# Down projection as seven half-size products with weight sums made in DRAM, and the out projection as four pairs of products, in a hybrid decoder block

## The chip, the cores and the metric

One core of one Trainium2 chip. The metric is the device time of one execution in microseconds, the median of several runs. TensorE (PE) multiplies, VectorE (DVE), ScalarE (ACT) and GpSimd (POOL) work element by element, SyncE (SP) issues most of the transfers; POOL issues the accumulating ones.

## The reference

A decoder block on 512 tokens with 16 learned meta tokens ahead, D = 1024, feed-forward width 2816. Two token mixers run in parallel (mLSTM and gated linear attention) and are merged by gates; then come an output projection, a second norm and a SwiGLU channel mixer. All products are asked for in float32. What matters here:

```python
xn = rmsnorm(h, norm1_g); proj = xn @ w_in        # mq mk mv mi mf mo gq gk gv ga gr gate_m gate_g
y_m = head_rmsnorm(mlstm_chunkwise(...)) * sigmoid(mo)
y_g = head_rmsnorm(gla_chunked(...)) * silu(gr)
merged = sigmoid(gate_m) * (y_m @ w_branch_m) + sigmoid(gate_g) * (y_g @ w_branch_g)
h = h + merged @ w_out
hn = rmsnorm(h, norm2_g)
ff = silu(hn @ w_ff_gate) * (hn @ w_ff_up)
h = h + ff @ w_ff_down
out = rmsnorm(h, final_g)
```

## The kernel before

Channels lie on the 128 partitions and tokens along the free dimension, so a tile of activations is 128 x 512 (or 528 with the meta tokens). A float32 product is made in three passes: weights and activations are each split into a high part (rounded by a cast on ACT) and a low part (the difference, on DVE), and high x high, high x low and low x high are summed in PSUM (`mm3`, L307 to L312).

Weights come in units of 128 x 1024 (512 KB, eight k-tiles of one output tile of 128 channels), loaded by SP (`load_raw`, L189) some units ahead into four buffers. `whi` (L196, ACT) and `wlo` (L201, DVE) split them. When a unit begins, `begin` (L279) hands out by tables (PLAIN, FIRST, SECOND) which splits of later units are emitted after which k-tile of the present one. Every other piece of work (norms, mixers, evacuations) is a Python generator in a list: `tick()` (L161), called after each k-tile, advances each by one step, and the number that it yields is how many ticks it then skips. So the order of the instructions on each engine is that of the program text, and the yields set it.

There are two kinds of job. A plain unit (`unit`, L316) makes one output tile with 24 matmuls of 512 columns. A pair (`pair`, L361, `seven`, L350) makes two output tiles by a scheme of the kind of Strassen's: with the weights as 2 x 2 blocks and the activations as 2 x 2 blocks, seven products of sums (q1, q5, q6, p2, p3, p4, p7), each half the size in k and in columns, 84 matmuls of 128 x 256 in all. p3 of a pair runs inside the next one. The sums of weights for pairs are made by accumulating DMAs that POOL issues (L191 into `raw`, L220 into `wf`) and by DVE (`s2` L235, `s4` L247); sums of the evacuated products are made by ACT and DVE, through a table of closures that a sink returns.

The stages: gates and mLSTM projections as plain units (0 to about 200 us); gates, GLA and the mLSTM's output as pairs, the branch units bm, and the mixers beside them (to about 480); eight branch units bg, whose result times gate plus the mLSTM's branch is the merged tile (`branch`, L1191 to L1204, to about 522); eight plain units out with the residual, the gain and the sum of squares behind each (L1358 to L1370, to about 568); the second norm (L1383), and, since all of the normed activations and their sums are needed (`operands`, L1416 to L1467), four plain gate and up units and then 18 pairs fg/fu with SwiGLU (L1488 to L1496, to about 792); the down projection, and the tail.

The down projection before takes 22 units of 512 KB, whose eight blocks of 128 x 128 follow a fixed list (output tiles 0 and 1 in turn for each of the 22 k-tiles, then tiles 2 to 7 one after the other). The activations are split once (L1525). Tiles 0 to 6 are 22 x 3 matmuls of 512 columns, tile 7 is done in two halves of 256 columns; after each tile its result is subtracted from the residual (L1570, the up branch carries a minus sign), squared for the last norm, and scaled by the gain. `final` (L1588) sums the squares over partitions by a matmul with ones, takes the root, and scales and stores the half that is done.

## Time and profile before

| | us |
|---|---|
| runs | 928.77 median of 3 (928.13 to 928.81) |
| the profiled execution | 928.98, its span 927.2 |
| PE busy | 912.5 (6145 matmuls in the record) |
| DVE busy | 631.0 |
| ACT busy | 539.0 |
| POOL busy | 90.4 |
| mean granted clock of PE | 0.995 |

A row of the groups gives line, engine, operation, output and inputs by name, shape and count, then busy us, mean ns of one, and the idle time ahead of it with what ended it. The waits list what PE waited for, with the total, the number and the longest in us. A row of a timeline has start, duration, engine, line and operation. The windows give busy us of each engine in a stretch, then the granted clock of PE (1.00 is full), the share of the 16 DMA engines' time that was used, and GB/s.

### The profile page before, as it was taken

How to read it: one execution, taken by the hardware profiler on the slowest of the kernel's cores; microseconds unless marked ns; L12 is line 12 of the kernel's file. 1: busy time of each engine (PE TensorE's matmuls, PEld its weight loads, DVE VectorE, ACT ScalarE, POOL GpSimd, SP SyncE). 2: the span in 40 equal slices, each digit the busy share in tenths (PEclk: the TensorE clock that was granted, in tenths of full speed). 3: DMA queues.
4: the chain of work that ended last, by engine and by line, in shares of the span. 5: the costliest groups of instructions: out<-in, count | busy, mean ns of one | idle time of the engine just before them, and what ended most of it. 6: DMA issues, size and time to landing. Idle time of an engine off the chain costs nothing.

```text
span 927.2 us, 15643 instructions
## 1 busy us (share of the span) xinstructions
PE 912.5 (98%) x6145; PEld 842.9 (91%) x6145; DVE 631.0 (68%) x937; ACT 539.0 (58%) x959; POOL 90.4 (10%) x109
## 2 busy tenths in 40 slices
PE   9999999999999999999999999999999999999995
PEld 9889999899998899999998888889999999888885
DVE  4889676888865487777786554997766767822323
ACT  6667568898774276767683334455555556722222
POOL 0000021111100011011100000141111210000000
PEclk9999999999999999999999999999999999999998
DMA  9255374465643567556543443357676775432302
GB/s 345 97 167 146 126 165 104 104 147 139 162 124 91 129 157 168 147 128 159 137 123 94 130 148 109 80 137 193 172 203 183 174 188 152 136 92 68 114 1 92
DMA packets 50650, 128.21 MB, mean 138 GB/s; under 512 B 5616, under 2 KB 11888, under 8 KB 50576
## 3 DMA queue, kind: packets, MB, share of 16 engines
q1 hardware_dynamic: 36224, 103.96, 35.4%
q0 software_dynamic: 13120, 22.16, 15.4%
q10 hardware_dynamic: 1232, 1.09, 0.4%
q8 instruction: 48, 0.79, 0.3%
q14 instruction: 26, 0.21, 0.1%
HBM read 121.82 MB, written 5.37 MB: 137 GB/s over the span
## 4 chain that ended last, share of the span: by engine, by line
PE 92%; DVE 5%; ACT 2%; issue 1%; DVEq 0%; POOL 0%; POOLq 0%
PE b L310 14%; PE b L312 14%; PE b L311 14%; PE b L356 14%; PE b L358 14%; PE b L357 14%; ACT t L140 1%; PE b L1153 1%; PE b L1152 1%; DVE wlo L201 1%; DVE t L1439 1%; PE b L1132 1%; PE b L824 1%; DVE hx L1446 1%; PE b L1173 1%
## 5 line engine op out<-in xcount | busy, mean ns | idle before, releaser
L311 PE MATMUL b<-t,whi 128*128 128x512 f32 (+2 forms) x790 | 277.4, 351 | 0.2 <-DVE t L925 0.2
L356 PE MATMUL b<-t,whi 128*128 128x256 f32 (+1 forms) x912 | 261.5, 287 | 0.9 <-ACT t L417 0.5
L310 PE MATMUL b<-t,whi 128*128 128x512 f32 (+2 forms) x742 | 261.1, 352 | 0.0
L312 PE MATMUL b<-t,wlo 128*128 128x512 f32 (+2 forms) x742 | 258.4, 348 | 2.2 <-DVE wlo L201 2.2
L358 PE MATMUL b<-t,wlo 128*128 128x256 f32 (+1 forms) x912 | 257.8, 283 | 0.7 <-DVE wlo L201 0.7
L357 PE MATMUL b<-t,whi 128*128 128x256 f32 (+1 forms) x912 | 257.3, 282 | 0.0
L201 DVE TENSOR_TENSOR wlo<-raw,whi 128x1024 fp32r<-128x1024 f32 x153 | 187.7, 1229 | 95.3 <-ACT whi L196 94.9
L196 ACT CAST whi<-raw 128x1024 fp32r<-128x1024 f32 x153 | 160.4, 1052 | 59.7 <-PE b L357 27.4
L356 PEld LDWEIGHTS b<-t,whi 128*128 128x128 f32 x912 | 171.9, 188 | 1.9 <-ACT t L417 0.8
L358 PEld LDWEIGHTS b<-t,wlo 128*128 128x128 f32 x912 | 171.7, 188 | 0.9 <-DVE wlo L201 0.9
L357 PEld LDWEIGHTS b<-t,whi 128*128 128x128 f32 x912 | 172.0, 189 | 0.4
L311 PEld LDWEIGHTS b<-t,whi 128*128 128x128 f32 x790 | 149.6, 189 | 20.8 <-DVE t L925 0.8
L312 PEld LDWEIGHTS b<-t,wlo 128*128 128x128 f32 x742 | 140.6, 189 | 21.0 <-DVE wlo L201 2.6
L310 PEld LDWEIGHTS b<-t,whi 128*128 128x128 f32 x742 | 140.8, 190 | 18.6
L140 ACT ACTIVATE t<-t 128x512 f32<-128x512 f32 (+7 forms) x133 | 76.1, 589 | 44.7 <-DVE t L1195 25.5
L191 POOL DMA_DIRECT2D raw<-wst x38 | 32.9, 866 | 369.8 <-DMA wf<-wst 122.6
L196 ACT CAST whi<-wf 128x1024 fp32r<-128x1024 f32 x38 | 40.0, 1053 | 19.9 <-PE b L357 15.4
L140 ACT ACTIVATE t<-f 128x256 f32<-128x256 f32 (+1 forms) x24 | 11.5, 481 | 62.0 <-DVE f L1570 62.0
L220 POOL DMA_DIRECT2D wf<-wst x38 | 37.4, 993 | 100.4 <-ACT whi L196 41.0
L201 DVE TENSOR_TENSOR wlo<-wf,whi 128x1024 fp32r<-128x1024 f32 x38 | 46.3, 1220 | 0.0
L1492 ACT COPY t<-b 128x256 f32<-128x256 f32 x54 | 18.5, 375 | 43.4 <-PE b L358 43.4
L356 PE MATMUL b<-t,wgh 128*128 128x256 f32 (+1 forms) x152 | 43.2, 284 | 0.0
(248 smaller groups left out, 1194.1 us busy)
## 6 DMA issues: line engine op xcount, KB each, us to landing
raw<-wst SPq DMA_DIRECT2D x153, 512.0 KB, 3.9
wf<-wst SPq DMA_DIRECT2D x38, 256.0 KB, 3.4
wf<-wst POOLq DMA_DIRECT2D x38, 256.0 KB, 6.3
raw<-wst POOLq DMA_DIRECT2D x38, 256.0 KB, 4.2
t<-xT SPq DMA_DIRECT2D x8, 264.0 KB, 5.3
pos<-t SPq DMA_DIRECT2D x8, 264.0 KB, 3.2
xt<-xr SPq DMA_DIRECT2D x4, 512.0 KB, 8.3
t<-xT SPq DMA_DIRECT2D x8, 256.0 KB, 3.9
```

What stands on the lines that cost most here:

```text
L140: S.activation(o, i, func, **kw)
L191: G.dma_start(lr(r, 0), lr(wst[v - 1], 0), accum_op=ALU.add)
L196: S.copy(t, src)
L201: V.tensor_tensor(t, src, hi.bitcast(F32), ALU.subtract)
L220: G.dma_start(lr(st.f, 1), lr(wst[u + 1], 1), accum_op=ALU.add)
L310: T.matmul(o, w_h, ah[:, c0:c1], start=first, stop=False)
L311: T.matmul(o, w_h, al[:, c0:c1], start=False, stop=False)
L312: T.matmul(o, w_l, ah[:, c0:c1], start=False, stop=last)
L356: T.matmul(o, h, xh_[k][:, c0:c1], start=start and k == 0, stop=False, skip_group_check=not start)
L357: T.matmul(o, h, xl_[k][:, c0:c1], start=False, stop=False, skip_group_check=not start)
L358: T.matmul(o, l, xh_[k][:, c0:c1], start=False, stop=k == 3, skip_group_check=not start)
L1492: s7=lambda: S.copy(s[:, lo], bz), s1=lambda: S.copy(s[:, hi], bx), s2=lambda: S.copy(r[:, lo], bx),
```

## The change

Out projection: the eight plain units become four pairs, of output tiles 2i and 2i+1. The merged tiles therefore have to be summed and split into seven operands (`upper_mix`, `lower_mix`, run behind the branch units, which now go 0, 4, 1, 5, 2, 6, 3, 7). The first pair goes over k = 0 to 2 of q1, p7 and p2 first, and then over k = 3. The residual's input is loaded a pair ahead, and sums of squares of four tiles are made by POOL with accumulating DMAs.

Down projection: one such scheme over the whole matrix. With two halves of the 22 k-tiles, of the tokens, and even against odd output tiles, there are seven products, each run for all four pairs of output tiles (4 x 11 x 3 matmuls of 256 columns) before the next. The result of each is added to or subtracted from the residual where it belongs, and three products accumulate into the banks of earlier ones. The activations' sums are made in place on DVE, one product ahead (`make_sum`), and split for each product (`make_op`). The weights come in 44 chunks of two k-tiles for all four pairs, each 512 KB or, at the odd end and for p3, 640 or 768 columns or half. The sums of weights are not made beside the use: `down_sums` makes them in DRAM, in 30 steps, each a copy from DRAM to DRAM (SP) and one job later an accumulating DMA (POOL). A step is advanced at each pair and at each odd bm or bg job, the rest in feed-forward pairs. The last twelve, for p3, pick rows of 512 B.

Many yields elsewhere have other numbers; the arithmetic there is the same.

```diff
@@ gate_rows, conv
         S.copy(gam[:96], gsb[:96])
...
-        yield 1
+        yield 2
...
         while not norm[0]:
-            yield 1
+            yield 6
...
+ORDER = ("q1", "q5", "p2", "p7", "q6", "p4", "p3")
+CHUNKS = [(n, 0, k, min(2, FH - k)) for n in ORDER[:-1] for k in range(0, FH, 2)] + [
+    ("p3", i, k, n) for i in range(4) for k, n in ((0, 6), (6, 5))]
...
+    def down_sums():
+        def plus(dst, a, b):
+            nc.sync.dma_start(dst, a)
+            yield
+            G.dma_start(dst, b, accum_op=ALU.add, max_dma_last_dim=8192)
+
+        for n, a, b in (("q5", wdn[2], wdn[3]), ("p7", wdn[2], wdn[0]), ("q6", dsum["q5"], wdn[0])):
+            for k in range(0, FH, 2):
+                c = slice(k, min(k + 2, FH))
+                yield from plus(dsum[n][c], a[c], b[c])
+        for i in range(4):
+            for k in range(0, FH, 4):
+                c = slice(k, min(k + 4, FH))
+                rows = lambda s: s[c, :, i * P:(i + 1) * P].rearrange("k p n -> p k n")
+                yield from plus(dsum["p3"][i].rearrange("p (k n) -> p k n", k=FH)[:, c], rows(dsum["q6"]), rows(wdn[1]))
...
+        if what in ("bm", "bg") and i % 2 or len(job) == 2:
+            next(sums, None)
...
+    def lower_mix(k):
+        b, b1, c = mo[k + 4].v, mo[k].v, mo[k].c
+        h = tt(F32R, NS)
+        act(h, b, AF.Copy, scale=0.5)
+        t = c[:, R2]
+        V.tensor_tensor(t, b[:, R2], b1[:, R2], ALU.subtract)
+        d = tt(n=NS)
+        V.scalar_tensor_tensor(d[:, L2], c[:, L2], -1.0, b[:, R2], ALU.mult, ALU.subtract)
...
+        lower(l, b, h)
+        put(("p2", "p3"), h, l)
+        V.scalar_tensor_tensor(d[:, R2], d[:, L2], -1.0, b[:, L2], ALU.mult, ALU.subtract)
...
+        lower(p_, t, p)
+        put(("p7",), p, p_)
+        yield 2
+        lower(dl, d, dh)
+        put(("q6", "p4"), dh, dl)
...
+        if last_k:
+            for b, n in ((bx, "q1"), (bz, "p7"), (by, "p2")):
+                seven(b, w, x, n, True, quiet, *cols, range(3))
+            while len(x["p7"][1]) < 4:
+                tick()
+            seven(bx, w, x, "q1", True, quiet, *cols, (3,))
+            e.pop("s1")()
+            mine["p3", 0] = ["s7"]
+            seven(by, w, x, "p2", True, quiet, *cols, (3,))
+            seven(bz, w, x, "p7", True, hook, *cols, (3,))
...
+            return dict(
+                s1=lambda: V.tensor_tensor(s[:, lo], bx, xa[:, lo], ALU.add),
+                s7=lambda: S.copy(s[:, hi], bz),
+                s2=lambda: V.tensor_tensor(r[:, lo], bx, xb[:, lo], ALU.subtract),
+                s5=lambda: V.tensor_tensor(r[:, hi], bx, xb[:, hi], ALU.subtract),
+                c21=lambda: minus(b[:, lo], bz, r[:, lo]),
+                c11=lambda: V.tensor_tensor(a[:, lo], by, s[:, lo], ALU.add),
+                c22=lambda: minus(b[:, hi], s[:, hi], r[:, hi]),
+                c12=lambda: V.tensor_tensor(a[:, hi], bx, xa[:, hi], ALU.add), fin=fin)
...
+    for i in range(4):
+        pair((("out", 2 * i), ("out", 2 * i + 1)), mg, (0, 256), sink_out(2 * i), i == 0)
...
-    for m in range(2, 7):
-        o = bank()
-        down(o, m, 0, NS)
-        run(out_res(m, o, 0, NS))
...
+    def make_op(n, k, part):
...
+        if part == 0:
+            make_sum(n, k)
+        elif part == 1:
+            xd[n][k] = tt(F32R, NS)
+            S.copy(xd[n][k][:, LO], src)
+        else:
+            V.tensor_tensor(xd[n][k][:, HI], src, xd[n][k][:, LO].bitcast(F32), ALU.subtract)
...
+    EVAC = {"q1": [(E, LO, -1, False)], "q5": [(O, HI, 1, False)], "p2": [(E, LO, -1, True)],
+            "p7": [(O, HI, 1, False)], "q6": [(E, HI, -1, False), (O, LO, 1, False), (O, HI, 1, True)],
+            "p4": [(O, LO, 1, True)], "p3": [(E, HI, -1, True)]}
+    INTO = {"q6": "q1", "p4": "p7", "p3": "q5"}
...
+        for step, (ws, xs_) in enumerate(((0, LO), (0, HI), (1, LO))):
+            T.matmul(o, w[ws][:, j * P:(j + 1) * P], xd[n][k][:, xs_], start=fresh and step == 0,
+                     stop=step == 2 and k == FH - 1, skip_group_check=True)
```

How the order moves, at three places. First DVE near the start, in the opening: `wlo` is the low part of the weight that PE uses about 44 us into the span; the narrow operations of 32 partitions belong to the gates' rows, the ones with `pr` and 528 or 512 columns to the convolution. Before:

```order
L678 TENSOR_TENSOR t_83_492<-b_65_410,t_41_183 128x512
L717 TENSOR_TENSOR a2s_343<-pr_69,a2s_343 32x512
L718 SCALAR_TENSOR_TENSOR t_78_462<-t_71_444,pr_69,t_77_461 32x528
L722 COPY t_85_510<-t_77_461 32x4
L723 SCALAR_TENSOR_TENSOR t_76_460<-t_85_510,t_78_462 32x528
L786 SCALAR_TENSOR_TENSOR t_73_454<-t_70_440,pr_69,t_73_454 128x512
L729 TENSOR_TENSOR t_87_524<-t_76_460,t_77_461 32x528
L730 TENSOR_SCALAR t_87_524<-t_87_524 32x528
L786 SCALAR_TENSOR_TENSOR t_79_464<-t_72_447,pr_69,t_79_464 128x528
L201 TENSOR_TENSOR wlo_88_535<-raw_58_232,whi_84_508 128x1024
```

The same place now (L833 is the convolution's L786, L220 is L201, L764 to L777 are L717 to L730):

```order
L833 SCALAR_TENSOR_TENSOR t_82_486<-t_78_467,pr_69,t_82_486 128x528
L220 TENSOR_TENSOR wlo_85_526<-raw_58_236,whi_84_507 128x1024
L833 SCALAR_TENSOR_TENSOR t_72_457<-t_70_444,pr_69,t_72_457 128x512
L764 TENSOR_TENSOR a2s_347<-pr_69,a2s_347 32x512
L765 SCALAR_TENSOR_TENSOR t_77_465<-t_71_448,pr_69,t_76_464 32x528
L769 COPY t_86_537<-t_76_464 32x4
L770 SCALAR_TENSOR_TENSOR t_75_463<-t_86_537,t_77_465 32x528
L776 TENSOR_TENSOR t_88_548<-t_75_463,t_76_464 32x528
L777 TENSOR_SCALAR t_88_548<-t_88_548 32x528
L833 SCALAR_TENSOR_TENSOR t_82_486<-t_78_467,pr_69,t_82_486 128x528
```

The low part has moved ahead of eight rows. Second, DVE where the down projection runs: before, in its first tiles, only low parts of activations of 512 columns and of weights.

```order
L1525 TENSOR_TENSOR t_1577_9160<-t_1248_6940,t_1575_9150 128x512
L1525 TENSOR_TENSOR t_1579_9170<-t_1267_7068,t_1578_9162 128x512
L1525 TENSOR_TENSOR t_1582_9182<-t_1286_7196,t_1580_9172 128x512
L1525 TENSOR_TENSOR t_1585_9194<-t_1305_7324,t_1583_9184 128x512
L201 TENSOR_TENSOR wlo_1587_9201<-raw_1545_8976,whi_1584_9189 128x1024
L1525 TENSOR_TENSOR t_1588_9206<-t_1324_7452,t_1586_9196 128x512
```

Now, in its first product, the sums for the next (L1672), their low parts (L1690), the weights' low parts, and at the end the evacuation into the residual (L1740):

```order
L1690 TENSOR_TENSOR t_1649_9643<-t_1323_7432,t_1649_9643 128x256
L1672 TENSOR_TENSOR t_1361_7688<-t_1361_7688 128x256
L1690 TENSOR_TENSOR t_1651_9661<-t_1342_7560,t_1651_9661 128x256
L1672 TENSOR_TENSOR t_1380_7816<-t_1380_7816 128x256
L220 TENSOR_TENSOR wlo_1655_9693<-raw_1642_9590,whi_1653_9675 128x1024
L1690 TENSOR_TENSOR t_1654_9681<-t_1361_7688,t_1654_9681 128x256
L1672 TENSOR_TENSOR t_1399_7944<-t_1399_7944 128x256
L1690 TENSOR_TENSOR t_1656_9699<-t_1380_7816,t_1656_9699 128x256
L220 TENSOR_TENSOR wlo_1660_9724<-raw_1647_9628,whi_1658_9713 128x1024
L1690 TENSOR_TENSOR t_1659_9719<-t_1399_7944,t_1659_9719 128x256
L1740 TENSOR_TENSOR f_1094_6237<-f_1094_6237,b_1627_9493 128x256
L220 TENSOR_TENSOR wlo_1666_9754<-raw_1652_9666,whi_1664_9737 128x1024
```

Between the weights' low parts, which keep their distance of a few rows, DVE now makes a sum and a low part of 256 columns for each k-tile. Third, POOL's queue at the pairs, before:

```order
L191 DMA raw_403_2271<-wst 128x512
L220 DMA wf_424_2334<-wst 128x512
L191 DMA raw_444_2448<-wst 128x512
L220 DMA wf_453_2477<-wst 128x512
L191 DMA raw_467_2607<-wst 128x512
```

and now, with the accumulating DMAs of the sums (L1222) between the weights':

```order
L198 DMA raw_408_2288<-wst 128x512
L239 DMA wf_424_2339<-wst 128x512
L1222 DMA sum_q5_191<-wdn 64x2048
L198 DMA raw_444_2455<-wst 128x512
L239 DMA wf_453_2484<-wst 128x512
L1222 DMA sum_q5_191<-wdn 64x2048
L198 DMA raw_467_2616<-wst 128x512
```

The copies that these add to (L1220) stand in the same manner between the loads on SP's queue.

More of the change, by code (lines that the diff above doesn't have):

```diff
@@ L108, in hybrid_block @@
 @with_exitstack
-def hybrid_block(ctx: ExitStack, tc: tile.TileContext, xT, xr, wst, par, con, out):
+def hybrid_block(ctx: ExitStack, tc: tile.TileContext, xT, xr, wst, wdn, par, con, out):
     nc = tc.nc
@@ L348, in hybrid_block, with seven @@
     SEVEN = ("q1", "q5", "q6", "p2", "p3", "p4", "p7")
-    def seven(o, w, x, n, start, hook, c0, c1):
+    def seven(o, w, x, n, start, hook, c0, c1, ks=range(4)):
         wh, wl = w[n]
         xh_, xl_ = x[n]
-        for k in range(4):
+        for k in ks:
             h, l = wh[:, k * P:(k + 1) * P], wl[:, k * P:(k + 1) * P]
@@ L754, in gate_rows @@
             yield 2
-        yield 11
+        yield 9
         pst = bank()
@@ L1198, in branch @@
         sg.v = None
-        yield 2
-        if parts is not None:
-            hi, lo = tt(F32R, NS), tt(F32R, NS)
-            act(hi, t, AF.Copy, scale=0.5)
-            yield 4
-            V.scalar_tensor_tensor(lo, t, 0.5, hi.bitcast(F32), ALU.mult, ALU.subtract)
-            parts[0].append(hi)
-            parts[1].append(lo)
-            box.v = None
+        if then is not None:
+            yield from then
+        yield 1
     ym, yg = [None] * 8, [None] * 8
@@ L1212, in hybrid_block @@
     gm, gg = [box() for _ in range(8)], [box() for _ in range(8)]
-    mg = [], []
+    mg = {n: ([], []) for n in SEVEN}
+    mo = [box() for _ in range(8)]
     heads = {}
@@ L1332, in hybrid_block @@
         elif what == "bg":
-            run(branch(box(), branch_unit(job[0], yg), gg[i], merged[i], mg))
-    while side:
-        tick()
+            if i == 3:
+                load_x(0)
+            run(branch(mo[i], branch_unit(job[0], yg), gg[i], merged[i],
+                       upper_mix(i) if i < 4 else lower_mix(i - 4)))
     del ym, yg, xh, xl, gts
@@ L1590, in final, with evac_out @@
+    INTO = {"q6": "q1", "p4": "p7", "p3": "q5"}
+    def evac_out(n, i):
+        for f, c, sign, last in EVAC[n]:
+            update(f(i), c, n, i, sign, last)
+            yield 2
+    def final(a):
+        while hsum[a].n < 8 - a:
+            yield 1
+        yield 1
         ps = bank()[:, :HS]
         for c in (slice(0, P), slice(P, HS)):
-            T.matmul(ps[:, c], ones, hsum[a].v[:, c], start=c.start == 0, stop=False, skip_group_check=True)
-        while o.v is None:
-            yield 1
@@ L1595, in final @@
-        yield from out_res(7, o.v, a * HS, (a + 1) * HS)
-        yield 1
-        for c in (slice(0, P), slice(P, HS)):
-            T.matmul(ps[:, c], ones, hsum[a].w[:, c], start=False, stop=True, skip_group_check=True)
+            T.matmul(ps[:, c], ones, hsum[a].v[:, c], start=c.start == 0, stop=a == 0, skip_group_check=True)
+        if a == 1:
+            while hsum[1].w is None:
+                yield 4
+            yield 9
+            for c in (slice(0, P), slice(P, HS)):
+                T.matmul(ps[:, c], ones, hsum[a].w[:, c], start=False, stop=True, skip_group_check=True)
@@ L1614, in final @@
             yield 1
[L1616 to L1635 removed]
+    flat = [0]
@@ new lines, in down_block @@
+    def down_block(n, i, k, cur):
+        o = out_of(n, i)
+        w = cur.w
+        j = cur.at
+        fresh = n not in INTO and k == 0 and i % 2 == 0
+        for step, (ws, xs_) in enumerate(((0, LO), (0, HI), (1, LO))):
+            T.matmul(o, w[ws][:, j * P:(j + 1) * P], xd[n][k][:, xs_], start=fresh and step == 0,
+                     stop=step == 2 and k == FH - 1, skip_group_check=True)
+        for f in cur.steps.get(j, ()):
+            f()
+        cur.at += 1
+        flat[0] += 1
+        if flat[0] % 2 == 0:
+            tick()
@@ new lines, in hybrid_block, with next_chunk, evac_all_out @@
+    unit_no = [0]
+    def next_chunk():
+        cur = Box()
+        name, _, _, size = CHUNKS[unit_no[0]]
+        u, steps = begin(("down", unit_no[0]))
+        top = (size if name == "p3" else 4 * size) - 1
+        cur.steps = {}
+        for at, fs in steps.items():
+            cur.steps.setdefault(min(at, top), []).extend(fs)
+        unit_no[0] += 1
+        cur.w, cur.at = splits.pop(u), 0
+        return cur
+    def evac_all_out(n):
+        for i in range(4):
+            yield from evac_out(n, i)
@@ new lines, in hybrid_block @@
+    for x, n in enumerate(ORDER):
+        if n in INTO:
+            acc[n] = acc.pop(INTO[n])
+        else:
+            acc[n] = [bank(), bank()]
+        nxt = ORDER[x + 1] if x + 1 < len(ORDER) else None
+        if n != "p3":
+            for k in range(FH):
+                if k % 2 == 0:
+                    cur = next_chunk()
+                for i in range(4):
+                    down_block(n, i, k, cur)
+                    if i == 0:
+                        make_op(nxt, k, 0)
+                    elif i == 2:
+                        make_op(nxt, k - 1, 2)
+                        make_op(nxt, k, 1)
+                if x == 0 and k == 0:
+                    left("p3", "c12", "fin")
+                xd[n][k] = None
+            make_op(nxt, FH - 1, 2)
+            run(evac_all_out(n))
+        else:
+            for i in range(4):
+                for k in range(FH):
+                    if k in (0, 6):
+                        cur = next_chunk()
+                    if i == 3 and k == 6:
+                        run(final(1))
+                    down_block(n, i, k, cur)
+                    if i == 1 and k == 0:
+                        run(final(0))
+                run(evac_out(n, i))
```

359 lines of the change are left out of this document (207 added, 152 removed).

## The prediction

> **What bounds the kernel now.** I read the page first: the span, the busy time of the engines, and the chain that ended last.
>
> ```profile
> span 927.2 us, 15643 instructions
> PE 912.5 (98%) x6145; PEld 842.9 (91%) x6145; DVE 631.0 (68%) x937; ACT 539.0 (58%) x959; POOL 90.4 (10%) x109
> PE 92%; DVE 5%; ACT 2%; issue 1%; DVEq 0%; POOL 0%; POOLq 0%
> ```
>
> TensorE is busy in 98% of the span and holds 92% of the chain, so the time is the sum of its matmuls, and what can be won elsewhere is small. The waits of PE come next: engine, line, what it waited for, then us in total, number of waits and the longest.
>
> ```profile
> PE b L312 <- DVE wlo L201: 2.2, 1, 2.2
> PE b L1173 <- POOL onesr L433: 1.0, 1, 1.0
> PE b L1598 <- ACT t L140: 1.0, 1, 1.0
> PE b L358 <- DVE wlo L201: 0.7, 1, 0.7
> ```
>
> The largest is one wait for a weight's low part. Then the pitch of the matmuls, which needs evenly spaced instructions that each follow one block of products. The first row is the residual after each of the eight output units (24 matmuls of 512 columns each), the second an evacuation in each of 18 feed-forward pairs (84 of 256 columns), the last two the evacuations of two output tiles of the down projection, four tiles of 66 matmuls of 512 columns apart.
>
> ```profile
> L1360 DVE TENSOR_TENSOR f<-b,t x8: 691/692/692, 529.7 to 568.6; 128x512 f32<-128x512 f32 x8
> L1494 DVE TENSOR_TENSOR t<-b,t x18: 418/420/425, 620.6 to 789.1; 128x256 f32<-128x256 f32 x18
> 838.83 0.69 DVE L1570 TENSOR_TENSOR f<-f,b 128x512 f32<-128x512 f32 x1 [8.95 <-PE b L312]
> 899.79 0.69 DVE L1570 TENSOR_TENSOR f<-f,b 128x512 f32<-128x512 f32 x1 [9.65 <-PE b L312]
> ```
>
> Out: 38.9 / 7 / 24 = 0.2316 us per 512-column matmul. Pairs: 168.5 / 17 = 9.91 us per pair, / 84 = 0.1180 us per 256-column matmul. Down: 60.96 / 4 / 66 = 0.2309 us. Two half-size matmuls cost 0.236, so halving loses 2% and seven eighths of the work gains 12.5%.
>
> **The change part by part.** The sum is made against the profiled run, 928.98 us (span 927.2); the median of the runs is 928.77.
>
> *Down, matmuls.* Before: 7 tiles x 22 x 3 = 462 of 512 columns, 462 x 0.2309 = 106.7 us, and 132 of 256, 15.6 us; together 122.3. After: 7 products x 4 pairs x 11 x 3 = 924 of 256 columns, 924 x 0.1180 = 109.0. **-13.2 us.** No cover is needed for this: the pairs of the feed-forward run at that pitch with a new weight for each matmul.
>
> *Out, matmuls.* Before 192 x 0.2316 = 44.5 us, after 4 x 84 x 0.1180 = 39.7. **-4.8 us.**
>
> *The wait near the start.* The retuned yields move the DVE instruction for which PE waits. Its time in the trace, with PE, DVE and ACT rows, and the windows around it (the columns are the window, then busy us of PE, PEld, DVE, ACT, POOL, then the granted clock, DMA share, GB/s):
>
> ```profile
> 44.05 0.39 PE L311 MATMUL b<-t,whi 128*128 128x512 f32 x1
> 46.64 0.51 PE L312 MATMUL b<-t,wlo 128*128 128x512 f32 x1 [2.21 <-DVE wlo L201]
> 40.23 0.68 DVE L717 TENSOR_TENSOR a2s<-pr,a2s 32x512 fp32r<-32x512 f32 x1
> 45.38 1.20 DVE L201 TENSOR_TENSOR wlo<-raw,whi 128x1024 fp32r<-128x1024 f32 x1
> 35.95 1.05 ACT L196 CAST whi<-raw 128x1024 fp32r<-128x1024 f32 x1
> 44.00:46.00 2.00, 0.43 (x2) 0.00 (x1) 1.97 (x4) 1.11 (x2) 0.00 (x0) 1.00 0.00 0
> 46.00:48.00 2.00, 1.36 (x4) 1.11 (x5) 1.94 (x4) 1.98 (x5) 0.00 (x0) 0.78 0.25 37
> 48.00:50.00 2.00, 2.00 (x6) 1.51 (x6) 1.55 (x4) 1.77 (x6) 0.00 (x0) 0.50 0.58 229
> 50.00:52.00 2.00, 2.00 (x9) 1.62 (x8) 2.00 (x3) 2.00 (x6) 0.00 (x0) 0.86 0.00 0
> ```
>
> PE's matmul of 44.05 is followed one pitch later, at 44.29, by nothing until 46.64: 2.35 us. Then the clock stands at 0.78, 0.50 and 0.86 for three windows of 2 us, which loses 2 x (0.22 + 0.50 + 0.14) = 1.7 us. In the new order the low part stands ahead of the eight rows that run from 40.23 to 45.38, and its high part has been there since 37.0. It would start at 40.2 and end at 41.4, 2.9 us before it is wanted. **-4.1 us** (0 to -4.1). Next late is the low part of the following unit, with about half a microsecond to spare by the same counting, which is why the lower end stays open.
>
> [...]
>
> *Entry into out.* The first pair needs the last two merged tiles split and mixed. DVE pitches for this and the next parts come from four rows of a stretch in which DVE runs back to back, and three groups give full durations (busy us, mean ns of one, then idle before).
>
> ```profile
> 588.68 0.68 DVE L1439 TENSOR_TENSOR t<-hx,t 128x512 fp32r<-128x512 f32 x1
> 589.28 0.68 DVE L1457 TENSOR_TENSOR t<-hx,hx 128x512 f32<-128x512 f32 x1
> 590.48 1.22 DVE L201 TENSOR_TENSOR wlo<-raw,whi 128x1024 fp32r<-128x1024 f32 x1
> 591.62 0.68 DVE L1462 TENSOR_TENSOR t<-t,hx 128x512 f32<-128x512 f32 x1
> L1193 DVE SCALAR_TENSOR_TENSOR t<-t,b 128x512 f32<-128x512 f32 x16 | 11.0, 688 | 30.9 <-PE b L312 30.9
> L1366 DVE SCALAR_TENSOR_TENSOR t<-f,pr,t 128x512 fp32r<-128x512 f32 x8 | 6.0, 748 | 0.8 <-ACT t L140 0.8
> ```
>
> So a 512-column operation blocks DVE for 0.60 us (589.28 - 588.68) and is done after 0.69; one of 1024 blocks 1.14 (591.62 - 590.48); for 256 columns I estimate 0.33 from these two, with 0.42 as the full duration (the L1494 row). After the last branch unit DVE must do three operations of 512 columns and four of 256 before the last operand of p7 stands: 3 x 0.69 + 4 x 0.42 = 3.75 us. The first pair runs q1, p7 and p2 over k = 0 to 2 and then q1 and p2 at k = 3 ahead of that, 33 matmuls, 3.9 us. Covered on paper; ACT's casts lie between, so **+0.3** (0 to 4.4, the upper end if the chain is not covered at all and one 512-column operation is added).
>
> *DVE within out.* A feed-forward pair takes 14.29 / 20 of DVE (the 640 window below), 7.1 us of 9.91. In an out pair three evacuations and a product go (-3 x 0.42 - 0.69), seven half evacuations come (7 x 0.42) and two scaled low parts (2 x 0.75): 9.6 us of 9.91 by full durations, some 9.1 by pitch. It fits with little left. **+0.5** (0 to 3). Residual loads of 256 KB ride on SP two per pair, and the squares go through POOL by accumulating DMA, where nothing waits for them before the norm.
>
> *Out into the first feed-forward unit.* After the last product DVE has a half evacuation, a weight's low part and one scaled operand: 0.42 + 1.22 + 0.75 = 2.4 us, against 9 matmuls of 512 columns, 2.1 us, that need none of it. **+0.3** (0 to 1).
>
> *DVE within down.* The activations are summed, split and evacuated per product: 44 sums, 66 low parts, 36 evacuations and 13 sums of squares, 159 operations of 256 columns, plus 5.5 weight chunks of 1024 in each of seven products. By pitch 159 x 0.33 + 38.5 x 1.14 = 96 us, by full durations 159 x 0.42 + 38.5 x 1.22 = 114 us, against 109 us of PE. The heaviest products (22 operations that prepare the next, 4 to 12 evacuations) take 13.6 to 15.9 us by pitch of PE's 15.6. The back-to-back rows are nearest, so pitch holds and the weights' lead of about two chunks of 2.85 us absorbs a late one: **+1.0** (0 to 5).
>
> *The weight sums.* Thirty steps, each a DRAM copy from SP and, a job later, an accumulating DMA from POOL. 28 of them lie where PE runs pairs and branch units. What they can disturb are the weights of those jobs; the rows below give the DMA share there, the price of packets by queue (packets, MB, share of 16 engines; the first two over 120 us, the third and fourth over 5 us each, one filled by accumulating 1-KB pieces and one by copies of 1.1-KB pieces), and one weight's way.
>
> ```profile
> 340.00:360.00 20.00, 20.00 (x167) 20.00 (x166) 15.10 (x22) 14.00 (x30) 3.68 (x5) 1.00 0.71 163
> 420.00:440.00 20.00, 20.00 (x175) 19.96 (x174) 14.49 (x22) 15.31 (x27) 3.46 (x4) 1.00 0.65 155
> 440.00:460.00 20.00, 20.00 (x169) 19.65 (x168) 16.05 (x27) 14.84 (x28) 1.73 (x2) 1.00 0.51 124
> 460.00:480.00 20.00, 20.00 (x161) 19.47 (x160) 13.87 (x22) 14.99 (x27) 1.72 (x2) 1.00 0.56 151
> 640.00:660.00 20.00, 20.00 (x172) 20.00 (x171) 14.29 (x21) 11.25 (x21) 4.42 (x6) 1.00 0.72 186
> q1 hardware_dynamic: 5184, 15.73, 39.9%
> q0 software_dynamic: 3456, 6.29, 32.4%
> q0 software_dynamic: 524, 0.54, 78.8%
> q1 hardware_dynamic: 1170, 1.38, 82.1%
> 356.90 0.86 POOL L191 DMA_DIRECT2D raw<-wst  x1 [8.90 <-DMA wf<-wst]
> 367.63 0.86 POOL L191 DMA_DIRECT2D raw<-wst  x1 [8.79 <-DMA wf<-wst]
> raw<-wst POOLq DMA_DIRECT2D x5, 256.0 KB, 4.5
> 366.65 1.06 ACT L196 CAST whi<-raw 128x1024 fp32r<-128x1024 f32 x1
> ```
>
> A pair job lasts 10.7 us (367.63 - 356.90); a share of 0.57 (mean of the three windows from 420) leaves 4.6 us of all 16 engines free in it, 0.71 leaves 3.1. The queues cost 0.399 x 1920 / 15.73 = 48.7 and 0.324 x 1920 / 6.29 = 98.9 engine-us per MB, so a step of 0.52 MB costs 77 engine-us, 4.8 us of 16 engines; with the add at the copy's price 3.2. A step of rows has 512 pieces of 512 B twice: at the 1-KB pieces' prices (0.821 x 80 / 1170 = 56 ns and 0.788 x 80 / 524 = 120 ns) 90 engine-us, 5.6 us; at half of them, 2.8. Six row steps fall into consecutive pair jobs. A weight issued at 356.90 lands 4.5 us later, at 361.4, and is first read at 366.65, so some 4.5 us of lateness is free. On SP's queue the copy stands ahead of the next weight, on POOL's the add stands behind a copy issued a job earlier, so POOL doesn't wait. **+0.5** (0 to 6: five large steps 1.7 over and six of rows 1.0 over, less the slack).
>
> *Tail.* The last product ends in the same chain of square, ones matmul, root, scale and store, per half: 0.
>
> Sum: -13.2 - 4.8 - 4.1 + 0.3 + 0.5 + 0.3 + 1.0 + 0.5 = -19.5, and 928.98 - 19.5 = **909.5 us**. Its own range is 906 to 913.
>
> **The rivals.** *Late weights through the sums.* The share of 0.71 speaks for it, the slack of 4.5 us against. Priced at the upper end it is +6, without the slack +15 (8.5 + 6.4): 915 to 924. Chance 0.12. [...]
>
> *DVE becomes the bound in down.* At full durations DVE needs 114 us for 109, and the heavy products 17.6 for 15.6, so PE waits 5 to 8 us: 914 to 917. The back-to-back rows speak against it, the dependence of each low part on an ACT cast of the same tile for it. Chance 0.12.
>
> *The start's wait isn't removed* but moves to the next low part: 909.5 + 4.1 = 913.6. Chance 0.05.
>
> *Slower: the row steps choke the queues.* If a piece of 512 B costs what the feed-forward's mean packet costs (0.399 x 1920 / 5184 = 148 ns and 0.324 x 1920 / 3456 = 180 ns), a row step takes 512 x 328 ns / 16 = 10.5 us against 4.6 free; six of them are 35.6 us over, less 4.5: 909.5 + 31 = 940. It takes all the gain from (19.5 + 4.5) / 6 + 4.6 = 8.6 us per step, 268 ns per piece for copy and add; the nearest row says 176. Chance 0.05 for slower; 0.03 that it comes out about even, so that the change as a whole does nothing at 928.
>
> **How the numbers follow.** Forecast 0.63. Faster 0.63 + 0.12 + 0.12 + 0.05 = 0.92, same 0.03, slower 0.05; 0.2% (1.9 us) is about what a measurement of this kernel can tell. The range goes from 905, a microsecond below the sum with all costs at zero (906.9), to 921, which leaves out the dearest part of the first rival and the slower cases.
>
> **What would show it.** Right: the evacuations of the seven products 15.6 us apart; the out pairs 9.9 us apart; no wait and a clock of 1.00 around 44 us; PE waits below 7 us in all. Wrong: waits of PE for weight low parts between 200 and 520 us with a DMA share near 1 (first and fourth rival), or for low parts of activations in down (second).

## The result, and the profile after

The changed kernel takes 913.1 us (median of four, 911.17 to 914.18) against 928.56; the ratio is 0.9827, 95% interval 0.9815 to 0.9839. Forecast were 909.5 us and a range of 905 to 921. The profiled execution is the fastest of the four, 911.17 us with a span of 909.4, 17.8 us below the profiled execution of before; the steps below are measured in it, and what the other executions add is a point of its own.

The page after, and PE's waits (line, what it waited for, us in total, times, longest):

```profile
span 909.4 us, 17138 instructions
PE 894.3 (98%) x6615; PEld 852.4 (94%) x6615; DVE 707.0 (78%) x1144; ACT 582.5 (64%) x1062; POOL 129.0 (14%) x151
```

```profile
PE b L381 <- DVE t L1516: 1.1, 2, 1.0
PE b L381 <- ACT t L1641: 1.1, 1, 1.1
PE b L1793 <- DVE f L1740: 1.0, 2, 0.5
PE b L1242 <- POOL onesr L480: 1.0, 1, 1.0
PE b L1767 <- ACT t L144: 0.5, 1, 0.5
```

PE is still busy in 98% of the span, with 18.2 us less to do. All its waits together are 6.1 us, below the 7 us that the prediction named as a sign of being right. The wait for a low part near 44 us is gone; in its place stand three smaller ones, at places that the change made or altered: an evacuation in out (L1516), the first feed-forward pair (L1641, where before had 0.7 us for a low part), the last product of down (L1740).

The windows at the start, to be held against those of before:

```profile
44.00:46.00 2.00, 2.00 (x10) 1.66 (x9) 1.93 (x4) 0.63 (x1) 0.00 (x0) 1.00 0.03 12
46.00:48.00 2.00, 2.00 (x10) 1.62 (x10) 1.94 (x4) 1.93 (x3) 0.00 (x0) 1.00 0.02 4
48.00:50.00 2.00, 2.00 (x13) 1.75 (x12) 1.97 (x3) 1.97 (x7) 0.00 (x0) 1.00 0.00 0
```

PE is busy throughout and the clock stays at 1.00. The branch units bg, which began at 477.54 us, begin at 473.43.

The down projection from its first matmul to the ones matmul that closes the last norm, before and then after:

```profile
791.46 0.39 PE L310 MATMUL b<-t,whi 128*128 128x512 f32 x1
917.71 0.71 PE L1598 MATMUL b<-t,ones 128*128 128x128 f32 x4 [0.96 <-ACT t L140]
```

```profile
785.29 0.40 PE L1793 MATMUL b<-t,whi 128*128 128x256 f32 x2
899.85 0.71 PE L1767 MATMUL b<-t,ones 128*128 128x128 f32 x4 [0.52 <-ACT t L144]
```

126.25 us have become 114.56: 11.7 less.

### The profile page after: what moved, and what is told of

Read it like the earlier page. It is cut to its first block, busy times and chain, and to the rows that moved or that the text cites. A ratio compares the mean times of both kernels' runs of the same rounds, so it can differ in the third digit from the quotient of the medians.

```text
span 909.4 us, 17138 instructions
## 1 busy us (share of the span) xinstructions
PE 894.3 (98%) x6615; PEld 852.4 (94%) x6615; DVE 707.0 (78%) x1144; ACT 582.5 (64%) x1062; POOL 129.0 (14%) x151
## 5 line engine op out<-in xcount | busy, mean ns | idle before, releaser
L381 PE MATMUL b<-t,whi 128*128 128x256 f32 (+1 forms) x1008 | 288.8, 286 | 3.1 <-DVE t L1516 1.1
L382 PE MATMUL b<-t,whi 128*128 128x256 f32 (+1 forms) x1008 | 284.6, 282 | 0.0
L220 DVE TENSOR_TENSOR wlo<-raw,whi 128x1024 fp32r<-128x1024 f32 (+2 forms) x175 | 209.1, 1196 | 91.0 <-ACT whi L215 90.7
L215 ACT CAST whi<-raw 128x1024 fp32r<-128x1024 f32 (+2 forms) x175 | 178.8, 1023 | 59.9 <-PE b L382 21.8
L381 PEld LDWEIGHTS b<-t,whi 128*128 128x128 f32 x1008 | 190.0, 188 | 4.8 <-DVE t L1516 1.5
L382 PEld LDWEIGHTS b<-t,whi 128*128 128x128 f32 x1008 | 190.1, 189 | 0.5
L383 PEld LDWEIGHTS b<-t,wlo 128*128 128x128 f32 x1008 | 189.9, 188 | 0.5 <-DVE wlo L220 0.5
L336 PE MATMUL b<-t,whi 128*128 128x264 f32 (+1 forms) x528 | 178.6, 338 | 0.2 <-DVE t L972 0.2
L335 PE MATMUL b<-t,whi 128*128 128x264 f32 (+1 forms) x480 | 162.2, 338 | 0.0
L337 PE MATMUL b<-t,wlo 128*128 128x264 f32 (+1 forms) x480 | 159.6, 332 | 0.0
L144 ACT ACTIVATE t<-t 128x512 f32<-128x512 f32 (+8 forms) x145 | 80.6, 573 | 53.2 <-DVE t L1316 22.8
L1793 PE MATMUL b<-t,whi 128*128 128x256 f32 x616 | 110.5, 282 | 1.0 <-DVE f L1740 1.0
L336 PEld LDWEIGHTS b<-t,whi 128*128 128x128 f32 x528 | 99.9, 189 | 11.8 <-DVE t L972 0.8
L335 PEld LDWEIGHTS b<-t,whi 128*128 128x128 f32 x480 | 91.1, 190 | 8.9 <-ACT t L967 0.3
L337 PEld LDWEIGHTS b<-t,wlo 128*128 128x128 f32 x480 | 90.8, 189 | 8.7
L1793 PEld LDWEIGHTS b<-t,whi 128*128 128x128 f32 x616 | 95.1, 189 | 1.4 <-DVE f L1740 1.4
L1793 PE MATMUL b<-t,wlo 128*128 128x256 f32 x308 | 86.8, 282 | 0.0
L1793 PEld LDWEIGHTS b<-t,wlo 128*128 128x128 f32 x308 | 58.3, 189 | 0.0
L215 ACT CAST whi<-wf 128x1024 fp32r<-128x1024 f32 x42 | 44.0, 1048 | 19.9 <-PE b L382 11.6
```

What stands on the lines that cost most here:

```text
L144: S.activation(o, i, func, **kw)
L215: S.copy(t, src)
L220: V.tensor_tensor(t, src, hi.bitcast(F32), ALU.subtract)
L335: T.matmul(o, w_h, ah[:, c0:c1], start=first, stop=False)
L336: T.matmul(o, w_h, al[:, c0:c1], start=False, stop=False)
L337: T.matmul(o, w_l, ah[:, c0:c1], start=False, stop=last)
```

## The experiments

Each ratio is against runs of the kernel before on the same chip. Three chips were used, on which the kernel before took 929.23, 929.04 and 929.46 us. The changed kernel was repeated on the first of them, and the runs on the other two are set against that repetition.

**The same kernel again.**

> The changed kernel once more, unaltered, as the measure for the other runs on this chip and for a second profile. Its executions so far lie between 911.2 and 914.2 us, the longer ones with a mean granted clock of 0.995 where the profiled one had 0.997. Theory A (the clock falls once in some executions, by about 0.002 x 910 = 1.8 us, behind one of the waits of PE in out or at the first feed-forward pair): a profile with 0.995 shows a window with a clock near 0.5 beside one of these waits. Rival B (the spread is not the clock: transfers of the sums land at other times): the clock windows look as in the first profile and the waits between 200 and 520 us differ. Median expected 913.1.

913.14 us (911.59 to 913.62; before 929.23). Its profile has a span of 910.7 and no fall of the clock ahead of the end. What differs are the waits: the one of 1.0 us in out is missing, the one at the first feed-forward pair is 1.7 in place of 1.1, and there are new ones of 0.4 (at 370 us) and 0.3 and 0.2 (at the norm). Theory A asked for a profile with 0.995, and this one has 0.996, so theory A was not put to its test. The mean clock turns out to be a poor sign of it: it also counts the half clock at the end of the span (from 903.6 us on in the first profile), and two executions of the run with the new order (below) have spans of 909.3 us, one at 0.997 and one at 0.994. Nor can a fall be the whole spread, since one execution here took 913.36 us at 0.997. Of theory B, only the wait at 370 us lies between 200 and 520 us, and the sums need not be its cause: without them (below) the executions lie as far apart. A part of the spread is outside the span: this profiled execution took 2.9 us more than its span, the first one 1.8. Another part of the spread is the moment at which the clock first rises. The table of windows gives matmuls of about equal size in brackets (first PE, then PEld); between 8 and 10 us there are 17 in one kernel's profile and 11 in another's, though all issue the same there:

```profile
8.00:10.00 2.00, 2.00 (x17) 2.00 (x16) 2.00 (x5) 1.82 (x3) 0.00 (x0) 1.00 1.00 347
```

```profile
8.00:10.00 2.00, 2.00 (x11) 2.00 (x10) 2.00 (x4) 1.94 (x4) 0.00 (x0) 1.00 1.06 405
```

The first is the run with the plain out projection below, the second the run of the opening alone. By the clock records the rise comes at 8.4 us in the one and at 11.1 in the other, 9.3 in the changed kernel's first profile. In that profile matmuls of 264 columns follow each other 0.22 us apart before the rise and 0.12 after, so by these two pitches each us of delay costs about half a us, an estimate. Differences below are therefore read from stretches within a profile as well as from medians, which by the same estimate carry about 1 us of this.

**The opening alone.** The kernel before with the yields of the opening:

```diff
@@ normed_x .. conv_act of before, 18 yields, as in the change
         while not norm[0]:
-            yield 1
+            yield 6
```

> The kernel before with the yields of the opening alone (the functions from the normed activations to the convolution), nothing else. Theory (the start step stands by itself): the wait of 2.2 us near 44 us and the fall of the clock behind it go, 928.6 - 4.2 = 924.4 us. Rival (the time is given back later, since the work that was moved behind is now late elsewhere): between 926 and 928.6.

925.65 us against 929.23: 3.6 less. No wait near 44 us is left, and nothing is given back: the branch units begin at 474.04 in place of 477.54 (3.5 less, in an execution whose clock rose at 11.1 us in place of 9.6, which hides 0.8 by that estimate), and from there to the end the two profiles agree within 0.4. The step stands by itself, at 3.6 in the medians and 4.3 with the rise of the clock taken out.

**The old down projection in the changed kernel.**

```diff
-    for i in range(len(CHUNKS)):
+    for i in range(22):
...
-            next(sums, None)
+            pass
...
-    for x, n in enumerate(ORDER):
+    for m in range(2, 7):
+        o = bank()
+        down(o, m, 0, NS)
+        run(out_res(m, o, 0, NS))
```

> The changed kernel with the down projection of before (22 units, 512-column matmuls), and so without the sums in DRAM; out pairs and yields as changed. Theory (the down step is worth what the two profiles show between their first and last matmul, 125.1 - 113.4 = 11.7 us, and the sums cost nothing): 913.1 + 11.7 = 924.8 us. By the prediction's own terms (13.2 - 1.0 for DVE - 0.5 for the sums): 924.8 too. Rival (the sums or the denser DVE cost some us that the stage does not show): 922 or less. Rival (the yields were tuned to the new down): 927 or more.

922.39 us (922.28 to 926.83, six executions) where 924.8 was expected, so 9.3 by the medians. In its profile the stretch from the first down matmul (784.99) to the last ones matmul (911.13) is 126.14 us, as before, against 114.56. The stage's 11.6 stands. The missing 2.3 pointed to the sums, so they were taken out by themselves:

**No sums in DRAM.** The products multiply by other weights of the same size.

```diff
-            nc.sync.dma_start(dst, a)
             yield
-            G.dma_start(dst, b, accum_op=ALU.add, max_dma_last_dim=8192)
...
+    dsum.update(q5=wdn[2], p7=wdn[2], q6=wdn[0])
+    dsum["p3"] = wdn[1].rearrange("k p n -> (k p n)").rearrange("(i p m) -> i p m", i=4, p=P)
```

> The changed kernel without the sums in DRAM: down_sums issues nothing, and the products q5, p7, q6 and p3 read single weight blocks of the same sizes in their place, so the down projection multiplies by the wrong weights. Theory A (the down projection of before made the changed kernel 9.3 us slower where the stage itself differs by 11.6, so the sums cost the difference through late weights in the mixers' pairs and the branch units): 913.1 - 2 = 911 us, fewer waits around 370, 547 and 570 us, and less spread. Theory B (the sums are free, the difference came from the clock): 913.1 within 0.5.

913.02 us against 913.14 for the changed kernel, and from the start of the branch units to the last ones matmul 426.2 us where the changed kernel's two profiles have 426.4 and 426.9. The sums are free to within a microsecond, theory B. So the sums are not what is missing from the 9.3 of the run before this one. Four of its six executions lie within 0.1 us of 922.4, while the median of the changed kernel's first four lies 1.9 us above its profiled one; between the two profiled executions the spans differ by 11.0 us (920.4 and 909.4). The old down is thus worth 11.6 in its stage, and the smaller difference of the medians comes from the executions' spread, whose cause stays open.

**The sums twice.** Each copy and each add also into a tile that nobody reads.

```diff
             nc.sync.dma_start(dst, a)
+            for e in more:
+                nc.sync.dma_start(e, a)
             yield
             G.dma_start(dst, b, accum_op=ALU.add, max_dma_last_dim=8192)
+            for e in more:
+                G.dma_start(e, b, accum_op=ALU.add, max_dma_last_dim=8192)
```

> The changed kernel with each copy and each accumulation of the weight sums issued a second time, into spare tiles in DRAM that nobody reads. Measured so far, a 512-KB step adds 60 engine-us and a step of 512-byte rows 3.2 us of all 16 engines, and the DMA share between 320 and 400 us is 0.90. Theory A (the limit is the engines' time, with slack up to a share near 1): another 0.25 there gives a demand of 1.15, 0.15 x 80 = 12 us over, less a slack of 4.5, so +5 to +12: 918 to 925 us, with waits of PE for weights between 320 and 400 us. Theory B (engines overlap packets, a share of 0.9 is not near the limit): 913 to 915.

925.95 us (923.41 to 931.19), 12.8 more. That is theory A, a little above its range of 918 to 925: the cover that suffices for one set of sums does not suffice for two. PE's waits, four windows (busy us of PE, PEld, DVE, ACT, POOL, then clock, DMA share, GB/s) and the chain behind the longest wait:

```profile
PE b L381 <- ACT t L465: 7.4, 4, 3.4
```

```profile
220.00:240.00 20.00, 19.67 (x157) 19.27 (x157) 15.25 (x24) 13.42 (x25) 7.77 (x10) 1.00 0.99 293
240.00:260.00 20.00, 16.55 (x127) 16.14 (x126) 13.35 (x20) 12.97 (x22) 3.38 (x4) 0.91 1.08 276
340.00:360.00 20.00, 18.91 (x150) 18.30 (x150) 15.48 (x24) 13.14 (x29) 4.51 (x6) 1.00 1.05 303
360.00:380.00 20.00, 19.09 (x154) 18.35 (x152) 10.70 (x15) 9.39 (x18) 5.69 (x7) 1.00 1.06 295
```

```profile
244.01 1.04 ACT L215 CAST whi<-raw 128x1024 fp32r<-128x1024 f32 x1 [6.93 <-DMA raw<-wst]
245.75 0.37 ACT L465 COPY t<-b 128x256 f32<-128x256 f32 x1
246.17 0.58 PE L381 MATMUL b<-t,whi 128*128 128x256 f32 x1 [3.40 <-ACT t L465]
```

The DMA share is between 0.99 and 1.08 (0.87, 0.86, 0.94 and 0.94 in the same windows of the changed kernel), ACT idles 6.9 us ahead of the cast of a weight that has not landed, and the copy of a PSUM bank for which PE waits is queued behind that cast. In this chain the late weight reaches PE by way of ACT's order, not by the matmul that uses it; the waits of this kind are 7.4 us, those for a weight's own low part 1.1. The longest came earlier than expected, at 246 us and not between 320 and 400. The clock falls with it: 0.91 over the 20 us from 240, and matmuls of 256 columns 0.21 us apart behind the wait (at 246.56, 246.77 and 246.98), where the pitch of pairs is 0.118. The doubled copies also stand ahead of weights on SP's queue; whether that order or the engines' time made the weights late is not separated by this run.

**The sums begun earlier.** Twelve of the steps at units of the opening.

```diff
-        if what in ("bm", "bg") and i % 2 or len(job) == 2:
+        if what in ("bm", "bg") and i % 2 or what in ("mk", "mo") or len(job) == 2:
```

> The changed kernel with twelve of the thirty steps of the sums begun in the opening, at the mk and mo units, where the DMA share is 0.5 to 0.6, so that the rest end sooner and the branch units, out and the first feed-forward pairs have none beside them. If theory A of the run without sums holds (late weights from 320 us on): 911 to 912 us. If the sums are free: 913.1. If the opening's own transfers (the mixed activations by way of DRAM, 100 to 200 us) are held up: 914 or more.

912.86 us (911.37 to 914.31): no difference that can be told, as the run without sums would have it. Its profile has a wait of 0.9 us near 176 us, at the sum of the mLSTM's denominator (L1086), and none at 370 or 547. The run without sums has 0.5 us at the same place, so that wait does not show that the sums hold up the opening's transfers.

**The old out projection in the changed kernel.**

```diff
-    for i in range(4):
-        pair((("out", 2 * i), ("out", 2 * i + 1)), mg, (0, 256), sink_out(2 * i), i == 0)
+    for m in range(8):
+        xr = tt(n=NS)
+        nc.sync.dma_start(xr, xT[m][:, NM:])
+        run(residual(m, unit_real(("out", m), mg[0], mg[1]), xr))
```

> The changed kernel with the out projection of before: eight plain units, branch units in their old order, residual, squares and norm as before; the new down projection and the yields stay. Theory by the stage in the profiles (branch units to first feed-forward pair 135.5 us with the old out, 132.8 to 133.2 with the new): 913.1 + 2.5 = 915.6 us. By the prediction's terms (4.8 less 1.1): 916.8. Rival (the out pairs' waits come from the sums' transfers and not from DVE): as the first, but the waits near 609 us go too and it is below 915.

913.23 us, where 915.6 was expected. By the medians the out pairs win nothing. The rival, that the waits of the out pairs come from the sums' transfers, falls by the run without sums, which has the wait at the first feed-forward pair in full (1.7 us). In the profile the stretch from the branch units to the end tells more. First and last rows, of this kernel and of the changed one (whose last row stands above):

```profile
472.94 0.40 PE L332 MATMUL b<-t,whi 128*128 128x512 f32 x1
901.81 0.71 PE L1748 MATMUL b<-t,ones 128*128 128x128 f32 x4 [0.52 <-ACT t L143]
```

```profile
473.43 0.40 PE L335 MATMUL b<-t,whi 128*128 128x512 f32 x1
```

428.9 us with plain units, 426.4 with pairs. The clock rose at 8.4 us here, at 9.3 there, which hides 0.5 by the same estimate. It was run again:

> The changed kernel with the out projection of before once more, unaltered, for a second profile and more executions. Theory (an execution's time carries a random part of up to 1.7 us from the moment at which the clock first rises, 8.4 to 11.1 us into the span, so medians of four differ by up to 1 us for nothing; between the start of the branch units and the last matmul this kernel's profile has 429.3 us, the changed kernel's 426.6 to 427.3): the stretch in the profile is 429.3 again, and the median of all executions is 1.5 to 2 above 913. Rival: the stretch is 427, and the first profile was an odd one.

913.44 us (912.88 to 914.20), and the stretch is 428.9 again (here to the start of the last four matmuls, in the expectation to the last of them). The median is 0.4 above 913, where 1.5 to 2 was expected. The nine executions of the plain form have a mean of 913.5, the eight of the changed kernel 912.9. So the out pairs win 2.0 to 2.5 us in the profiles and 0.6 in the mean of the executions. The profiles of the changed kernel are those of 911.17 and 913.62 us; which waits the executions between them had was not recorded, and the last microsecond of this stays open.

**The last product's order.** 

```diff
-            for i in range(4):
+            for i in (0, 2, 1, 3):
```

> The changed kernel with the four pairs of the last product taken in the order 0, 2, 1, 3 in place of 0, 1, 2, 3, weights likewise, so that neighbours lie in different banks. Theory (the two waits of 0.5 us in the last product, at 885 and 894 us, come from the evacuation of the bank's other half, 0.7 us lost each): 913.1 - 1.4 = 911.7 us. Rival (DVE is late there anyway): 913.1, the waits stay or move to the next pair.

911.12 us (910.86 to 911.62) against 913.14: both waits for L1740 are gone and none came in their place. From the first matmul of down (786.50) to the last ones matmul (899.54) the profile has 113.04 us for 114.56, 1.5 less where 1.4 was expected; the profile does not show the rest of the 2.0. In the changed kernel the wait looks like this (PE and DVE):

```profile
885.97 0.51 PE L1793 MATMUL b<-t,whi 128*128 128x256 f32 x2 [0.52 <-DVE f L1740]
885.50 0.75 DVE L1740 TENSOR_TENSOR f<-f,b 128x256 f32<-128x256 f32 x2
```

Pair 1 of the last product writes the second half of the bank whose first half DVE is just reading for pair 0.

**That, and the first feed-forward pair.** The wait at 609 us in the changed kernel, rows of DVE, ACT and PE:

```profile
608.77 0.68 DVE L1552 TENSOR_TENSOR t<-b,t 128x512 f32<-128x512 f32 x1
609.48 0.63 ACT L144 ACTIVATE t<-t 128x512 f32<-128x512 f32 x1 [1.35 <-DVE t L1552]
610.02 0.63 ACT L1641 COPY t<-b 128x256 f32<-128x256 f32 x2
610.42 0.39 PE L381 MATMUL b<-t,whi 128*128 128x256 f32 x1 [1.09 <-ACT t L1641]
```

ACT stands in the Silu of the last plain unit, whose input DVE makes behind the operands of the pairs; the copies that free PE's banks are queued behind that Silu.

```diff
         while rs2.v is None:
             yield 7
+        if m == NSTD - 1:
+            while len(xw["p3"][1]) < 4:
+                yield 1
+            yield 3
```

> The changed kernel with the last product's pairs in the order 0, 2, 1, 3 (which gave 911.1) and with the SwiGLU of the last plain gate and up units held back until the operands of the pairs are all emitted and three ticks more, so that ACT copies the first pair's PSUM banks ahead of that Silu. Theory (PE's wait of 1.25 to 1.8 us near 609 us is ACT standing in a Silu that waits for DVE, which works off operands): the wait there falls to the copy itself, about 0.7 with what follows, and the time to 911.1 - 1.1 = 910.0 us. Rival (DVE's operands are themselves late, whatever ACT does): the wait moves to a low part of an operand behind it, 911.1.

909.86 us (908.93 to 910.89), ratio to before 0.9791 (0.9778 to 0.9804): the fastest version here. The wait for the copy is gone; one for the next low part of a weight is left:

```profile
PE b L381 <- ACT t L465: 1.3, 2, 0.9
PE b L1242 <- POOL onesr L480: 1.0, 1, 1.0
PE b L383 <- DVE wlo L220: 0.9, 1, 0.9
```

Near 610 us 1.81 and 0.46 us were lost in the run with the new order alone, and 1.1 is now; the medians differ by 1.3. With the out projection of before:

> The run of both improvements with the out projection of before (eight plain units). Theory (the out pairs win about 3.7 us of TensorE time up to the first feed-forward pair, of which 0.6 to 1.1 is given back in the wait at 609 us): that wait is already short here, so the difference from the run with out pairs is larger than between the kernels without the improvements, 2.5 to 3.5 us: 912.5 to 913.5 us. Rival (the out pairs win nothing, as the two medians of 913.1 and 913.2 read): the same time within 0.6.

911.91 us, 2.05 more than with pairs. In the two profiles (plain, then pairs):

```profile
474.22 0.40 PE L332 MATMUL b<-t,whi 128*128 128x512 f32 x1
901.04 0.71 PE L1752 MATMUL b<-t,ones 128*128 128x128 f32 x4 [0.52 <-ACT t L143]
```

```profile
474.14 0.40 PE L335 MATMUL b<-t,whi 128*128 128x512 f32 x1
897.19 0.71 PE L1771 MATMUL b<-t,ones 128*128 128x128 f32 x4 [0.52 <-ACT t L144]
```

426.8 against 423.1, a difference of 3.8 where it was 2.5 without the improvements. It would be easy to put the growth down to the Silu held back, as the expectation did, but the start of the first feed-forward pair says otherwise. Its first matmul in the changed kernel, the one with the plain out projection, and the two improved ones (pairs, then plain):

```profile
606.34 0.28 PE L381 MATMUL b<-t,whi 128*128 128x256 f32 x1
608.29 0.28 PE L378 MATMUL b<-t,whi 128*128 128x256 f32 x1
605.86 0.28 PE L381 MATMUL b<-t,whi 128*128 128x256 f32 x1
609.64 0.28 PE L378 MATMUL b<-t,whi 128*128 128x256 f32 x1
```

From the first branch unit to here the two plain kernels take 135.4 us, the changed kernel 132.9 and the improved one 131.7: 2.5 and 3.7 less. From here to the last ones matmul pairs and plain units agree within 0.1 in both cases (293.5 and 293.5, 291.3 and 291.4): the first pair loses 0.55 us less in the plain kernels, and their later pairs are 9.95 us apart in place of 9.91. So the 1.2 us more were won ahead of the Silu that was held back, where the two kernels with pairs issue the same; the wait of 1.0 us at L1516 is simply missing in this execution. The medians differ by 2.05, less than the stretches, and less than the 2.5 to 3.5 expected.

## Why the prediction was right, point by point

The sum was 19.5 us below the profiled execution of before; 17.8 was measured in the profiled execution.

*Down* (forecast 13.2 less 1.0 for DVE): 11.7. The pitch held. The first evacuations of the first and the fifth product are four products apart:

```profile
804.65 0.41 DVE L1740 TENSOR_TENSOR f<-f,b 128x256 f32<-128x256 f32 x1
866.52 0.42 DVE L1740 TENSOR_TENSOR f<-f,b 128x256 f32<-128x256 f32 x1
```

61.9 / 4 = 15.5 us per product, 15.6 by the sum. DVE kept up by its pitch (16.9 to 20.0 us busy in each 20 us between 800 and 880), and the second rival did not come. The 1.0 us charged to it was lost, 1.4 in fact, but not to DVE's load: to the last product's neighbours in one bank, which the prediction had not seen. That the charge was nearly of the right size is luck.

*The start* (forecast 4.1): 4.1 in the profiles, 3.6 to 4.3 in the run of the opening alone. It was right to count the clock of 0.78, 0.50 and 0.86 in the windows behind the wait as won too: the stall alone, 2.35 us, would not make up what came.

*Out* (forecast 4.8 less 1.1, so 3.7): this is the term that was mis-sized for the profiled execution. From the first branch unit to the first feed-forward pair the profile gives 132.9 us for 135.4 before, 2.5 less. The pairs of out are further apart than 9.91 us; the evacuation that PE waits for comes four times:

```profile
L1516 DVE TENSOR_TENSOR t<-b,t x4: 417/418/418, 526.7 to 557.4; 128x256 f32<-128x256 f32 x4
```

30.7 us for three pairs, 1.0 more than by pitch. That microsecond is one wait, and its chain begins with a weight (SP's issue, then ACT, DVE and PE):

```profile
540.11 0.33 SPq L194 DMA_DIRECT2D raw<-wst  x1
543.31 1.05 ACT L215 CAST whi<-raw 128x1024 fp32r<-128x1024 f32 x1 [2.44 <-DMA raw<-wst]
544.39 1.23 DVE L220 TENSOR_TENSOR wlo<-raw,whi 128x1024 fp32r<-128x1024 f32 x1 [2.04 <-ACT whi L215]
548.08 0.42 DVE L1516 TENSOR_TENSOR t<-b,t 128x256 f32<-128x256 f32 x1
548.55 0.38 PE L381 MATMUL b<-t,whi 128*128 128x256 f32 x1 [0.98 <-DVE t L1516]
```

DVE idles 2.0 us for the weight and then has 3.7 us of work ahead of the evacuation. The prediction had DVE nearly full there (9.6 of 9.91) and charged 0.5, with up to 3 in its range. In the other profiles with out pairs this wait is 0.2 us or not there, and the same stretch shows what else can come: the norm. The prediction let the squares go through POOL by accumulating DMA and charged nothing, because nothing waits for them before the norm. The norm does wait (DVE and PE in the run with the new order alone):

```profile
568.67 0.69 DVE L1487 TENSOR_TENSOR t<-t,t 128x512 f32<-128x512 f32 x1 [2.29 <-DMA t<-t]
570.79 0.50 PE L1539 MATMUL b<-t,onesr 128*128 128x512 f32 x1 [0.82 <-ACT t L1535]
```

In the run without sums, the one with the old down and the improved one, where neither wait costs more than 0.3 us, the stretch takes 131.6 to 131.7 us, 3.7 less than before: the forecast's own figure. With the one or the other it takes 132.8 to 133.2. The run with the sums begun earlier lies between (132.6), with 0.2 to 0.4 us lost at each of the two places.

*The first feed-forward pair* (not priced): PE loses 1.25 and 0.46 us there against 0.84 before, and the stretch from this pair to the first matmul of down is 0.4 longer. The prediction closed this part of its sum at the first feed-forward unit and did not ask what is late in the first pair, where DVE makes the operands.

*The sums* (forecast 0.5, up to 6): nothing that can be told. The prices lay at the lower side of the bounds. Queues between 404 and 484 us before, and between 400 and 480 after, where six row steps are added (packets, MB, share of 16 engines):

```profile
q1 hardware_dynamic: 2712, 8.29, 33.1%
q0 software_dynamic: 1440, 2.62, 21.2%
```

```profile
q0 software_dynamic: 4372, 4.10, 38.8%
q1 hardware_dynamic: 5126, 9.59, 37.3%
```

0.176 x 1280 us / 2932 packets = 77 ns for a piece's add and 0.042 x 1280 / 2414 = 22 ns for its copy: 99 ns, between the half price of 88 and the 176 of 1-KB pieces, and far from the 268 at which the slower rival decides. A row step takes 3.2 us of 16 engines. Transfers of the sums can make weights late all the same, as the run with the sums twice shows; one set more and 12.8 us of the gain are gone. With the copies from SP and the adds from POOL both doubled, the DMA share, 0.86 to 0.94 in four windows of the changed kernel, rose to between 0.99 and 1.08 there, and the weights came late.

*The tail* (forecast 0): 9.55 us from the last ones matmul to the end after, 9.49 before.

*From the profiled execution to the median.* The forecast was made against one execution, and the median of the changed kernel lies 1.9 us above its profiled one, where before's lay 0.2 below. Of the 3.6 us by which 913.1 is above the forecast, 1.7 is the terms above and 1.9 this. In those 1.7, out lacks 1.2, down 0.5 and the first feed-forward pair 0.4, and the 0.5 charged for the sums, which was not needed, hides a part of it. The waits that come and go between profiles (0 to 1.1 us at 547, 0 to 1.5 lost at the norm, 1.3 to 1.8 at 609) have about that size; which of them the longer executions had was not recorded.

## What to carry to other kernels

Where one engine is busy in 98% of the span, matmul counts times the pitch of a like stage gave each part of the change within a few tenths of a us, once the waits were counted apart; then follow the won time to the next places where another engine or a transfer was just in time, and look which engine's queue stands between. Here it paid to queue copies that free a bank ahead of work whose input is late (909.86 for 911.12 us), and to put products that follow each other into different banks (911.12 for 913.14). A median of four executions can hide two microseconds, so compare stretches within profiles, from one matmul to another, too, and split a stretch before you say which edit won it: a wait that is missing in one execution looks just like a gain.

## What the runs showed of the hardware

In the profile of before the clock records have three stretches within the work: full clock for 37.55 us, half clock for 3.41 us from 47.13 us on, and full clock for 870.40 us. The half clock came behind the wait of PE of 2.2 us near 44 us; matmuls of 512 columns are 0.43 us apart in it (47.70 to 48.13) and 0.23 after it (50.63 to 50.86). With the sums twice the clock was 0.91 between 240 and 260 us, where PE had waited 3.4 us. The changed kernel's first profile has waits of 1.0 and 1.1 us, and its clock record is one stretch at full clock of 894.29 us; the run without sums has a wait of 1.7 us at the same mean clock, 0.997. What a fall depends on was not shown. The first rise came at 8.4 us into the span with the plain out projection, at 9.3 in the changed kernel, at 9.6 in before and at 11.1 in the run of the opening alone, though all issue the same there; by the pitches of 0.22 and 0.12 us around it, these 2.7 us move everything behind by 1.2 us, an estimate.
